# Stick-breaking attention: the sum over keys taken by parts

## The chip, the cores and the metric

The kernel runs on one NeuronCore of one Trainium2 chip. The metric is device microseconds (us) from one execution to the next of the same program. All times below are of this core; engines are named PE or TensorE (matrix products), DVE or VectorE, ACT or ScalarE, POOL or GpSimd, and SP or SyncE, whose queue issues all the kernel's DMA transfers.

## What is computed

Two layers of a decoder trunk on a sequence of 1024 tokens with 1024 channels, in float32. In each layer three groups of heads read the same stream: A (differential attention, four heads of width 128), B (forgetting attention, four heads of 64) and C (stick-breaking attention, four heads of 64). Their outputs, each times a SiLU gate, go through one output projection, and a residual and a layer norm follow. The change concerns group C, of which the reference reads, cut to what matters:

```python
def _stick_breaking_attention(q, k, v):
    ...
        strict = kpos[None, :] < qpos[:, None]
        z = jnp.einsum('bhqd,bhkd->bhqk', qb, k).astype(jnp.float32) * scale
        log_fail = jnp.where(strict, jax.nn.log_sigmoid(-z), 0.0)
        after = lax.cumsum(log_fail, axis=3, reverse=True) - log_fail
        weights = jnp.where(strict, jnp.exp(jax.nn.log_sigmoid(z) + after), 0.0)
        return jnp.einsum('bhqk,bhkd->bhqd', weights.astype(v.dtype), v)
```

With f_j = sigmoid(-z_j) and F_j the product of f over the keys from j up to the query's own position, the weight of key j is sigmoid(z_j) F_(j+1), which is F_(j+1) - F_j.

## The kernel before

**Staging.** Each layer starts with the projections of v, q and k for group C (`START`: vC0, qC0, kC0), then walks through `FOLLOW`: for each pair of heads of C (C0, C1), head of A (A0 to A3) and pair of B (B0, B1) it runs the attention and, woven into it, the projections that later units need (for C0: qC1, kC1 and vA0) and the gates of finished ones. The output projection and the norm end the layer.

**A projection** is a chain of matmuls over eight slices of 128 channels, each with three products (high and low parts of weights and stream). Its weights come by DMA into `wraw` (three buffers) and are split by ScalarE (line 133) and GpSimd (line 134). The result lands in one of two PSUM banks "acc" and is evicted by ScalarE and VectorE. v of group C is a tile of 128 partitions (position within a block) x 8 blocks x 256 columns, written block by block by ScalarE (line 212). After a q projection eight DMA transfers make copies of it with the two partition halves swapped (lines 191 and 192), which the scores need.

**Attention by blocks.** A pair of C has eight blocks of 128 queries, i = 0 to 7, with n = 128 (i + 1) keys. Each block passes three stages:

- `soft`: TensorE computes the scores (line 254, four PSUM banks "S"); for each of the two heads ScalarE takes sigmoid(-z) into f (line 369) and sigmoid(z) into w (line 370); VectorE turns f into running products from the right with a scan over the reversed row (line 372; the mask puts the 1 at the diagonal); GpSimd clears the last column of w (line 373); VectorE multiplies w by f moved one column (line 374). f and w lie in the four buffers "e", so one block takes all four.
- `turn`: TensorE transposes w in pieces of up to 512 columns into PSUM banks "T" (two banks, line 274); ScalarE copies the first piece (line 276), VectorE the second (line 278).
- `mix`: TensorE multiplies with v into a bank "T"; VectorE copies the 128 columns to y (line 390).

`LAG` makes `turn` follow one step and `mix` two steps behind `soft`. `ORDER` gives the order of the stages within one step, as indices: 0 is `soft`, 1 `turn`, 2 `mix`. For C it is (4, 3, 2, 1, 0): mix of block i-2, turn of block i-1, soft of block i. For A and B, soft comes before turn. `advance` runs one step; how often is set by the costs that the stages return (`SCORE_US`, `PACE`), against the costs of the projections woven in.

**What sets the order in the queues.** The program is written with a tile framework. It fixes each engine's queue when the program is built: among the instructions that it expects to be ready, the one written first goes first, so that one written later can be placed ahead of one that is expected to wait. On the chip each engine then works through its queue in that order. A buffer tag (`bufs`, `pbufs`) has a fixed number of slots, and a tile that takes a slot waits for the last reader of the tile before it. `tc.issue_after` holds the transposes of the output stage behind a matmul.

Of the kernel before, what the change touches and what calls it, by code (L numbers as in the profile page):

```python
# [10 lines left out]
AF = mybir.ActivationFunctionType  # L11
ALU = mybir.AluOpType
# [3 lines left out]
P = 128  # L16
D = 1024
S = 1024
NB = S // P
NK = D // P  # L20
DEPTH = 2
HALF = 512
# [18 lines left out]

PACE = 8.0
LAG = (0, 1, 2, 3, 5)
ORDER = {"A": (4, 3, 2, 0, 1), "B": (4, 3, 2, 0, 1), "C": (4, 3, 2, 1, 0)}
PARTNER = list(range(8, 16)) + list(range(8)) + list(range(16, 32))


# [1 line left out]
def tile_trunk(ctx, tc, x, ln_in_g, ln_in_b, w_in, b_forget, lambda_q1, lambda_k1, lambda_q2,  # L49
               lambda_k2, subln_g, w_out, ln_g, ln_b, c_ident, c_mask, c_tri, c_rope, out):  # L50
    nc = tc.nc
# [10 lines left out]
    def big(tag, name, shape=(P, S), dt=F32):  # L62
        return sb.tile(list(shape), dt, tag=tag, name=name, bufs=bufs[tag])

    def bank(tag, name, shape=(P, HALF)):
        return ps.tile(list(shape), F32, tag=tag, name=name, bufs=pbufs[tag])
# [6 lines left out]
    ident = const.tile([P, P], F32, name="ident")  # L73
# [4 lines left out]
    y_dram = [dr.tile([D, S], F32, name=f"y_dram{l}") for l in range(DEPTH)]  # L78
    c_dram = [dr.tile([NB * 4, P], F32, name=f"c_dram{l}") for l in range(DEPTH)]

    # ---------------------------------------------------------------- layer norm
    def pieces(n):
        return [slice(a * D // n, (a + 1) * D // n) for a in range(n)]

# [42 lines left out]
            nc.scalar.copy(hs, t3)  # L127
            nc.vector.tensor_tensor(lo[:, 4 * n:4 * n + 4, cols], t3, f32(hs), ALU.subtract)

    # ---------------------------------------------------------------- weights  # L130
    def split_w(raw, shape, key, tags):
        hi, lo = big(tags[0], f"whi_{key}", shape, F32R), big(tags[1], f"wlo_{key}", shape, F32R)
        nc.scalar.copy(hi, raw)
# [11 lines left out]
            res += [(hi[:, j, :], lo[:, j, :]) for j in range(kn)]  # L145
        return res

    # ---------------------------------------------------------------- projections
    def proj_cols(hts, w, evac, key):
        for half in range(2):  # L150
            hhi, hlo = hts[half]
# [93 lines left out]
                done(res)  # L245
        yield from proj_cols(hts, load_w(layer, col, P, key, tags=tags), evac, key)

    # ---------------------------------------------------------------- attention
    def scores(i, kst, q1, q2, key):
        half, rows = i // 4, slice((i % 4) * P, (i % 4 + 1) * P)  # L250
        res = []
# [96 lines left out]
    def attn_pair(layer, kind, pair, kst, q1, q2, v, y, negc=None):  # L348
        key = f"{kind}{layer}{pair}"
        ws, wts = {}, {}  # L350

        def soft(i):
            n = (i + 1) * P
            for s in range(2):
                k2 = f"{key}_{i}_{s}"
                sc = scores(i, kst[s], q1[s], q2[s], k2)
                if kind == "B":
                    diag = negc[s][:, n - P:n]
                    nc.gpsimd.tensor_tensor(diag, diag, mask[:, D:], ALU.add)  # L359
                    w = big("e", f"e_{k2}")  # L360
                    nm = neg_max(sc, negc[s], w, k2)
                    z = tiny.tile([P, 1], F32, tag="z2", name=f"z2_{k2}")
                    nc.scalar.activation(w[:, :n], w[:, :n], AF.Exp, bias=nm, scale=-1.0, accum_out=z)  # L363
                    nc.vector.reciprocal(z, z)
                    nc.vector.tensor_scalar(w[:, :n], w[:, :n], z, None, ALU.mult)
                else:
                    f, w = big("e", f"f_{k2}"), big("e", f"s_{k2}")
                    for a, b, p in sc:
                        nc.scalar.activation(f[:, a:b], p, AF.Sigmoid, scale=-1.0)  # L369
                        nc.scalar.activation(w[:, a:b], p, AF.Sigmoid)  # L370
                    fr = f[:, :n][:, ::-1]
                    nc.vector.tensor_tensor_scan(fr, fr, mask[:, :n], 0.0, ALU.mult, ALU.max)  # L372
                    nc.gpsimd.memset(w[:, n - 1:n], 0.0)
                    nc.vector.tensor_tensor(w[:, :n - 1], w[:, :n - 1], f[:, 1:n], ALU.mult)
                ws[i, s] = w
            return 2 * SCORE_US[i]

        def turn(i):
            wts[i] = [transposed(ws.pop((i, s)), i, f"{key}_{i}_{s}") for s in range(2)]
            return 0.22 * (i + 1)  # L380

        def mix(i):
            wt = wts.pop(i)
            o = bank("T", f"O_{key}_{i}")
            for j in range(i + 1):
                for s in range(2):
                    vc = (2 * pair + s) * 64
                    mm(o[64 * s:64 * s + 64, :P], lhsT=v[:, j, vc:vc + 64],
                                     rhs=wt[s][:, j * P:(j + 1) * P], start=j == 0, stop=j == i)
            nc.vector.tensor_copy(y[:, i * P:(i + 1) * P], o[:, :P])  # L390
            return 0.24 * (i + 1)

        order = range(NB) if kind == "C" else range(NB - 1, -1, -1)
        return [(i, soft, turn, mix, None, None) for i in order]

    # ---------------------------------------------------------------- small per-layer quantities
    def layer_scalars(layer):
        lam_init = 0.8 - 0.6 * math.exp(-0.3 * layer)
        ex = []
# [50 lines left out]
            negc.append(m.rearrange("p b s -> p (b s)"))  # L450
        return negc

    # ---------------------------------------------------------------- output projection
    OUT_ORDER = (6, 7, 0, 1, 2, 3, 4, 5)

    def load_wout(layer):
# [45 lines left out]
            nc.vector.scalar_tensor_tensor(r[:, c0:c1], r[:, c0:c1], ALPHA, acc, ALU.mult, ALU.add)  # L502
        return r

    # ---------------------------------------------------------------- the trunk
    nc.vector.memset(mhalf, -0.5)
    hts = new_ht("0")
    xs = [big("e" if blk < 4 else "K", f"x_{blk}") for blk in range(NB)]
# [36 lines left out]
    for layer in range(DEPTH):  # L545
        got, vs, ys, extra = {}, {}, {}, {}

        def project(step, tags=("whi", "wlo")):
            op, kind, n = step[0], step[1], int(step[2])
            u = step[1:]  # L550
            key = f"{op}{kind}{layer}{n}"
            if op in "qk":
                def done(res):
                    got[step] = res
                    if op == "q":
                        got["2" + u] = swapped(res, key, (1, 0) if kind == "B" else (0, 1))
                yield from proj_heads(layer, hts, COLS[op][kind] + P * n, op == "q", key,
                                      extra["rope"] if kind == "A" else None, done, tags)
            elif op == "v":
                col, width = {"C": (CV, 256), "A": (AV + P * n, 256), "B": (BV, 260)}[kind]  # L560
                fx = None
                if kind == "B":
                    xt = tiny.tile([P, NB * 4], F32, tag="fx", name=f"fx_{layer}", bufs=1)
                    fx = (xt, extra["bias"])
                vs[u] = vs[f"{kind}{n + 1}"] = yield from proj_v(
                    layer, hts, col, width, key, fx, wv0 if layer == 0 and kind == "C" else None)
                if kind == "B":
                    extra["negc"] = forget(layer, xt)
            else:
                y = ys.pop(u)  # L570
                yield from proj_gate(layer, hts, COLS["g"][kind] + P * n, y, key)
                if u != "B1":
                    e = EBASE[kind] + n
                    nc.sync.dma_start(y_dram[layer][e * P:(e + 1) * P, :], y)
                    return
                extra["ylast"] = yl = (big("wT", f"ylhi_{layer}", (P, S), F32R), big("wT", f"yllo_{layer}", (P, S), F32R))
                for a in range(2):
                    cs = slice(a * HALF, (a + 1) * HALF)
                    nc.scalar.copy(yl[0][:, cs], y[:, cs])
                    nc.vector.tensor_tensor(yl[1][:, cs], y[:, cs], f32(yl[0][:, cs]), ALU.subtract)  # L580
# [14 lines left out]
        for n, tag in enumerate(("cos", "sin")):  # L595
            t = big(tag, f"{tag}_{layer}")
# [6 lines left out]
        def advance():  # L603
            nonlocal cursor
            cost = 0.0
            for stage in ORDER[pipe[min(cursor, len(pipe) - 1)][0][0]]:
                lag = LAG[stage]
# [10 lines left out]
        for u, steps in FOLLOW.items():  # L618
            kind, m = u[0], int(u[1])
            key = f"{kind}{layer}{m}"  # L620
            q1, kst, q2 = got.pop("q" + u), got.pop("k" + u), got.pop("2" + u)
            y = ys[u] = big("y", f"y_{key}")
            if kind == "A":
                blocks = attn_a(layer, m, kst, q1, q2, vs[u], (m % 2) * P, y, nlam, sg)
            else:
                blocks = attn_pair(layer, kind, m, kst, q1, q2, vs[u], y,
                                   extra["negc"][2 * m:2 * m + 2] if kind == "B" else None)
            pipe += [(u, blk) for blk in blocks]
            fill_all = sum({"v": 21.0}.get(st[0], 10.4) for st in steps)
            attn_all = NB * PACE + 2 * sum(SCORE_US) + (0.33 if kind == "A" else 0.46) * 36  # L630
            filled = attended = 0.0
            for step in steps:
                if step[0] == "g":
                    while finished.get(step[1:], 0) < NB:
                        attended += advance()
                for cost in project(step):
                    filled += cost
                    while cursor < len(pipe) and attended / attn_all < filled / fill_all:
                        attended += advance()
            while cursor < len(pipe):  # L640
                advance()
# [5 lines left out]
        for blk in range(NB):  # L647
            key = f"o{layer}{blk}"
# [54 lines left out]
```

## Time and profile before

| | |
|---|---|
| time, median of 3 runs | 1409.74 us (1407.7 to 1410.52) |
| span of the profiled execution | 1405.8 us |
| TensorE busy | 1335.0 us (95%) |
| VectorE busy | 921.9 us (66%) |
| ScalarE busy | 600.7 us (43%) |
| GpSimd busy | 320.3 us (23%) |
| data moved by DMA | 109.28 MB on the kernel's queue |

The profile is one execution taken by the hardware profiler; its span runs from the first to the last instruction. Its own time outside the profiler was not measured apart; the median of the runs stands 3.9 us above its span. "L372" is line 372 of the kernel. In the names, buffer numbers are left out: `f_C` is every f of group C. Helpers record their lines: every matmul is L71, every transpose of `turn` L274.

### The profile page before, as it was taken

How to read it: one execution, taken by the hardware profiler on the slowest of the kernel's cores; microseconds unless marked ns; L12 is line 12 of the kernel's file. 1: busy time of each engine (PE TensorE's matmuls, PEld its weight loads, DVE VectorE, ACT ScalarE, POOL GpSimd, SP SyncE). 2: the span in 40 equal slices, each digit the busy share in tenths (PEclk: the TensorE clock that was granted, in tenths of full speed). 3: DMA queues.
4: the chain of work that ended last, by engine and by line, in shares of the span. 5: the costliest groups of instructions: out<-in, count | busy, mean ns of one | idle time of the engine just before them, and what ended most of it. 6: DMA issues, size and time to landing. Idle time of an engine off the chain costs nothing. (4 is left out here: it accounts for less than half of the span.)

```text
span 1405.8 us, 22162 instructions
## 1 busy us (share of the span) xinstructions
PE 1335.0 (95%) x8218; PEld 1134.1 (81%) x8218; DVE 921.9 (66%) x1990; ACT 600.7 (43%) x1381; POOL 320.3 (23%) x372
## 2 busy tenths in 40 slices
PE   5999989999999999999999998899999999999997
PEld 5878767987888888778898796689788888877886
DVE  7656687749775675856532657974787567757555
ACT  2445454435344544641214544544453455546200
POOL 3411211122112222223413211211111122221332
PEclk9999999999999999999999999999999999999999
DMA  7520211121213122243433111111212141232332
GB/s 266 161 76 16 56 36 53 39 75 46 61 35 103 49 76 60 91 147 121 139 108 90 46 46 39 40 51 33 80 45 62 27 113 51 71 98 98 126 129 90
DMA packets 111404, 110.70 MB, mean 79 GB/s; under 512 B 8576, under 2 KB 89408, under 8 KB 111296
## 3 DMA queue, kind: packets, MB, share of 16 engines
q1 hardware_dynamic: 111296, 109.28, 26.6%
q8 instruction: 65, 1.06, 0.3%
q14 instruction: 43, 0.35, 0.1%
HBM read 72.52 MB, written 19.96 MB: 66 GB/s over the span
## 5 line engine op out<-in xcount | busy, mean ns | idle before, releaser
L71 PE MATMUL aco_o<-wo,yhi_o 128*128 128x512 f32 (+1 forms) x462 | 142.0, 389 | 0.0
L295 ACT ACTIVATE e_A<-e_A,nm_A 128x256 f32<-128x256 f32 (+7 forms) x128 | 98.8, 773 | 31.2 <-DVE nm_A L263 30.3
L372 DVE TENSOR_TENSOR_SCAN f_C<-f_C,mask 128x128 f32<-128x128 f32 (+7 forms) x64 | 94.1, 1473 | 26.9 <-ACT f_C L369 26.7
L71 PEld LDWEIGHTS aco_o<-wo,yhi_o 128*128 128x128 f32 x462 | 85.4, 188 | 19.1
L71 PE MATMUL acr_vvA<-whi_vvA,hT 128*128 128x256 f32 x512 | 94.7, 283 | 0.0
L71 PE MATMUL aco_o<-wo,ylo_o 128*128 128x512 f32 (+1 forms) x231 | 89.7, 388 | 0.0
L71 PE MATMUL S_A<-K_kA,Q_qA 128*128 128x384 f32 (+3 forms) x384 | 85.5, 356 | 0.0
L71 PE MATMUL acc_qA<-hT,whi_qA 128*128 128x512 f32 x256 | 84.0, 408 | 0.0
L71 PE MATMUL acc_kA<-hT,whi_kA 128*128 128x512 f32 x256 | 83.5, 407 | 0.0
L71 PE MATMUL acc_ggA<-hT,whi_ggA 128*128 128x512 f32 x256 | 82.2, 400 | 0.0
L71 PEld LDWEIGHTS acr_vvA<-whi_vvA,hT 128*128 128x128 f32 x512 | 80.5, 190 | 0.3
L274 PE MATMUL T_C<-ident,s_C 128*128 128x128 f32 x288 | 51.4, 301 | 29.9 <-DVE y_C L390 27.4
L71 PEld LDWEIGHTS O_A<-v_vA,wT_A 128*128 128x128 f32 x576 | 72.3, 191 | 3.4
L71 PE MATMUL O_A<-v_vA,wT_A 128*128 128x128 f32 x576 | 74.6, 275 | 0.0
L327 ACT ACTIVATE sq_A<-ou_A 128x128 f32<-128x128 f32 x64 | 19.9, 311 | 125.2 <-DVE ou_A L316 125.1
L71 PE MATMUL acr_vvA<-wlo_vvA,hT 128*128 128x256 f32 x256 | 72.3, 282 | 0.0
L274 PEld LDWEIGHTS T_C<-ident,s_C 128*128 128x128 f32 x288 | 34.5, 150 | 44.7 <-issue 24.9
L263 DVE CUSTOM_DVE_ANT_0 e_A<-S_A,mask 128x512 f32<-128x512 f32 (+3 forms) x128 | 68.5, 554 | 2.6 <-PE S_A L71 1.1
L485 POOL TENSOR_TENSOR ylo_o<-yr_o,yhi_o 128x256 fp32r<-128x256 f32 (+2 forms) x48 | 40.6, 875 | 117.1 <-ACT yhi_o L484 114.8
L71 PEld LDWEIGHTS S_A<-K_kA,Q_qA 128*128 128x128 f32 x384 | 62.5, 189 | 4.9 <-issue 0.7
L363 ACT ACTIVATE e_B<-e_B,nm_B 128x1024 f32<-128x1024 f32 (+7 forms) x64 | 49.5, 775 | 30.7 <-DVE nm_B L263 30.7
L359 POOL TENSOR_TENSOR negc<-negc,mask 128x128 f32<-128x128 f32 x64 | 34.1, 535 | 116.6 <-DVE nm_B L263 89.3
(212 smaller groups left out, 3556.9 us busy)
## 6 DMA issues: line engine op xcount, KB each, us to landing
Q_qA<-Q_qA SPq DMA_DIRECT2D x64, 128.0 KB, 2.9
wor<-in_w_out_dram SPq DMA_DIRECT2D x32, 256.0 KB, 2.8
r_o<-h_dram SPq DMA_DIRECT2D x16, 512.0 KB, 3.2
h_dram<-x SPq DMA_DIRECT2D x8, 512.0 KB, 3.7
wr_vvA<-in_w_in_dram SPq DMA_DIRECT2D x16, 256.0 KB, 2.8
Q_qC<-Q_qC SPq DMA_DIRECT2D x32, 128.0 KB, 2.3
wr_qA<-in_w_in_dram SPq DMA_DIRECT2D x16, 256.0 KB, 2.9
wr_kA<-in_w_in_dram SPq DMA_DIRECT2D x16, 256.0 KB, 3.0
```

The costliest lines, as they stand in the source:

```text
L71: recent[0] = nc.tensor.matmul(*args, **kw).ins
L263: nc.vector.tensor_tensor_reduce(e[:, a:b], sc, other[:, a:b], -1.0, lowest, ALU.add, ALU.min, nm)
L274: nc.tensor.transpose(out=t[:, c:c + P], in_=w[:, a + c:a + c + P], identity=ident)
L295: nc.scalar.activation(e[:, :n], e[:, :n], AF.Exp, bias=nm, scale=-1.0, accum_out=z)
L327: nc.scalar.activation(t[:, b * P:(b + 1) * P], ou[:, b, :], AF.Square, scale=P ** -0.5, accum_out=ss[:, b:b + 1])
L359: nc.gpsimd.tensor_tensor(diag, diag, mask[:, D:], ALU.add)
L363: nc.scalar.activation(w[:, :n], w[:, :n], AF.Exp, bias=nm, scale=-1.0, accum_out=z)
L372: nc.vector.tensor_tensor_scan(fr, fr, mask[:, :n], 0.0, ALU.mult, ALU.max)
L485: nc.gpsimd.tensor_tensor(ylo[:, e0:e0 + en, :], raw, f32(yhi[:, e0:e0 + en, :]), ALU.subtract)
```

## The change

The sum over keys is taken by parts. Since the weight is F_(j+1) - F_j, the sum of weights times v_j is the sum over j of F_j (v_(j-1) - v_j), plus v at the query's own position, with v_(-1) = 0. So the scan's result itself is transposed and multiplied, not by v but by differences of v, and y starts as v transposed.

- `soft` of C: one sigmoid and the scan stay; the second sigmoid, the memset and the multiply go. One "e" buffer per block and head instead of two.
- `ORDER["C"]` becomes (4, 3, 2, 0, 1): in one step, soft of block i comes before turn of block i-1.
- `mix` of C multiplies with `dv` (through `vs`) and adds the PSUM block to y instead of copying it.
- The new function `by_parts` runs once per layer, right after the last instruction of the projection vC0 in the program's order (in layer 0 that generator is finished after those of q and k were run through). It takes a second "v" buffer `dv`, clears its first row, and fills it with v one position down by two DMA transfers on SP's queue: partitions 0 to 126 to partitions 1 to 127 (8 KB each), and partition 127, blocks 0 to 6, to partition 0, blocks 1 to 7 (7 KB). For each pair it transposes v (eight 128 x 128 blocks, through two "T" banks), copies it to y with ScalarE (two copies of 512 columns), and subtracts v from `dv` on VectorE (128 partitions x 8 x 128). Both y tiles of C are taken there.

```diff
-ORDER = {"A": (4, 3, 2, 0, 1), "B": (4, 3, 2, 0, 1), "C": (4, 3, 2, 1, 0)}
+ORDER = {"A": (4, 3, 2, 0, 1), "B": (4, 3, 2, 0, 1), "C": (4, 3, 2, 0, 1)}
...
                 else:
-                    f, w = big("e", f"f_{k2}"), big("e", f"s_{k2}")
+                    w = big("e", f"f_{k2}")
                     for a, b, p in sc:
-                        nc.scalar.activation(f[:, a:b], p, AF.Sigmoid, scale=-1.0)
-                        nc.scalar.activation(w[:, a:b], p, AF.Sigmoid)
-                    fr = f[:, :n][:, ::-1]
+                        nc.scalar.activation(w[:, a:b], p, AF.Sigmoid, scale=-1.0)
+                    fr = w[:, :n][:, ::-1]
                     nc.vector.tensor_tensor_scan(fr, fr, mask[:, :n], 0.0, ALU.mult, ALU.max)
-                    nc.gpsimd.memset(w[:, n - 1:n], 0.0)
-                    nc.vector.tensor_tensor(w[:, :n - 1], w[:, :n - 1], f[:, 1:n], ALU.mult)
                 ws[i, s] = w
...
-            nc.vector.tensor_copy(y[:, i * P:(i + 1) * P], o[:, :P])
+            yc = y[:, i * P:(i + 1) * P]
+            if kind == "C":
+                nc.vector.tensor_tensor(yc, yc, o[:, :P], ALU.add)
+            else:
+                nc.vector.tensor_copy(yc, o[:, :P])
             return 0.24 * (i + 1)
...
+    def by_parts(layer, v, ys):
+        dv = big("v", f"dv_{layer}", (P, NB, 256))
+        nc.gpsimd.memset(dv[0:1, 0, :], 0.0)
+        nc.sync.dma_start(dv[1:P], v[0:P - 1])
+        nc.sync.dma_start(dv[0:1, 1:NB, :], v[P - 1:P, 0:NB - 1, :])
+        for pair in range(2):
+            cs = slice(pair * P, (pair + 1) * P)
+            y = ys[f"C{pair}"] = big("y", f"y_C{layer}{pair}")
+            for half in range(2):
+                t = bank("T", f"vt_{layer}{pair}{half}")
+                for b in range(4):
+                    nc.tensor.transpose(out=t[:, b * P:(b + 1) * P], in_=v[:, 4 * half + b, cs], identity=ident)
+                nc.scalar.copy(y[:, half * HALF:(half + 1) * HALF], t)
+            nc.vector.tensor_tensor(dv[:, :, cs], dv[:, :, cs], v[:, :, cs], ALU.subtract)
+        return dv
...
                 if kind == "B":
                     extra["negc"] = forget(layer, xt)
+                elif kind == "C":
+                    vs["C0"] = vs["C1"] = by_parts(layer, vs[u], ys)
...
-            y = ys[u] = big("y", f"y_{key}")
+            y = ys[u] if kind == "C" else big("y", f"y_{key}")
+            ys[u] = y
```

## Rows read from the trace of the kernel before

**Rows 1.** The page: span, and TensorE's busy time, share, instructions.
```profile
span 1405.8 us, 22162 instructions
...
PE 1335.0 (95%) x8218; PEld 1134.1 (81%) x8218; DVE 921.9 (66%) x1990; ACT 600.7 (43%) x1381; POOL 320.3 (23%) x372
```

**Rows 2.** Windows: length, busy us (instructions) per engine, clock, DMA share, GB/s.
```profile
80.00:232.00 152.00, 137.26 (x921) 114.50 (x920) 109.64 (x142) 77.02 (x172) 25.56 (x46) 0.96 0.17 42
768.00:922.00 154.00, 138.81 (x939) 115.84 (x938) 107.45 (x142) 76.68 (x170) 26.54 (x45) 0.97 0.16 42
232.00:768.00 536.00, 527.98 (x3185) 450.94 (x3184) 336.57 (x829) 223.87 (x522) 128.40 (x131) 1.00 0.28 82
110.00:120.00 10.00, 7.21 (x51) 6.60 (x50) 7.16 (x8) 5.18 (x12) 2.69 (x3) 0.83 0.22 52
```

**Rows 3.** Waits of PE over the span: us in total, times, longest.
```profile
PE T_C L274 <- DVE y_C L390: 27.4, 16, 3.0
```

**Rows 4.** Timeline, 218 to 229 us: start, duration, engine, instruction [idle before].
```profile
218.28 2.29 DVE L372 TENSOR_TENSOR_SCAN f_C<-f_C,mask 128x1024 f32<-128x1024 f32 x1 [0.54 <-ACT f_C L369]
...
220.68 1.23 DVE L374 TENSOR_TENSOR s_C<-s_C,f_C 128x1023 f32<-128x1023 f32 x1
...
221.82 3.39 DVE L372 TENSOR_TENSOR_SCAN f_C<-f_C,mask 128x1024 f32<-128x1024 f32 x1
...
225.35 2.01 DVE L374 TENSOR_TENSOR s_C<-s_C,f_C 128x1023 f32<-128x1023 f32 x1
...
228.60 0.28 DVE L390 COPY y_C<-O_C 128x128 f32<-128x128 f32 x1
...
228.93 1.08 PE L274 MATMUL T_C<-ident,s_C 128*128 128x128 f32 x4 [3.04 <-DVE y_C L390]
```

**Rows 5.** Groups by line: count | busy us, mean ns | idle before.
```profile
L374 DVE TENSOR_TENSOR s_C<-s_C,f_C 128x127 f32<-128x127 f32 (+7 forms) x64 | 53.2, 834 | 5.4 <-ACT s_C L370 0.5
...
L370 ACT ACTIVATE s_C<-S_C 128x384 f32<-128x384 f32 (+3 forms) x96 | 49.6, 517 | 4.0 <-DVE s_C L374 4.0
...
L373 POOL MEMSET s_C<- 128x1 f32 x64 | 6.3, 99 | 210.3 <-ACT s_C L370 208.5 <-DMA Q_qA<-Q_qA 1.9
```

**Rows 6.** Timeline of PE: eight transposes in a row.
```profile
725.04 1.03 PE L124 MATMUL ht_ps_o<-ident,r_o 128*128 128x128 f32 x8
```

**Rows 7.** Groups by line and shape: VectorE's largest multiply, ScalarE's 512-column copy.
```profile
L374 DVE TENSOR_TENSOR s_C<-s_C,f_C 128x1023 f32<-128x1023 f32 x8 | 11.4, 1421 | 0.9
...
L276 ACT COPY wT_C<-T_C 128x512 f32<-128x512 f32 x40 | 23.4, 585 | 40.8 <-PE T_C L274 38.8 <-ACT wT_C L276 1.6
```

**Rows 8.** DMA: the data queue (packets, MB, share); issues by KB, us to landing.
```profile
q1 hardware_dynamic: 111296, 109.28, 26.6%
...
h_dram<-r_o SPq DMA_DIRECT2D x8, 512.0 KB, 2.6
...
c_dram<-cs SPq DMA_DIRECT2D x2, 16.0 KB, 1.4
```

**Rows 9.** Timeline of SP's queue around the ends of v, both layers.
```profile
66.24 2.86 SPq L143 DMA_DIRECT2D wr_vvA<-in_w_in_dram  x3
69.19 0.52 SPq L191 DMA_DIRECT2D Q_qC<-Q_qC  x1
...
742.00 1.63 SPq L143 DMA_DIRECT2D wr_qC<-in_w_in_dram  x2
744.50 2.81 SPq L143 DMA_DIRECT2D wr_kC<-in_w_in_dram  x2
```

**Rows 10.** Timeline of ACT: the last copies of v, both layers.
```profile
66.30 0.37 ACT L212 COPY v_vC<-acr_vvC 128x256 f32<-128x256 f32 x1
...
742.05 0.37 ACT L212 COPY v_vC<-acr_vvC 128x256 f32<-128x256 f32 x1
```

**Rows 11.** Timeline of PE: the first scores, both layers.
```profile
77.99 0.45 PE L71 MATMUL S_C<-K_kC,Q_qC 128*128 128x128 f32 x3
...
764.73 0.56 PE L71 MATMUL S_C<-K_kC,Q_qC 128*128 128x128 f32 x4
```

## The prediction

> **What bounds the kernel now.** I read the page's busy list first, then windows, then the waits of TensorE, then timelines. TensorE is busy 1335.0 of 1405.8 us [rows 1], so only its waits, its clock and the work given to it can move the time. The windows say where it waits [rows 2]: the two stretches in which group C's attention runs (80 to 232 us in layer 0, 768 to 922 us in layer 1). There TensorE is idle for 14.7 and 15.2 us, and its granted clock is 0.96 and 0.97, which is worth another 0.04 x 152 + 0.03 x 154 = 10.7 us at full speed. The 536 us between them hold 8.0 us of idle time and a clock of 1.00. So what better flow in group C can return is 29.9 + 10.7 = 40.6 us at most.
>
> Most of that idle time has one cause: 27.4 us in 16 waits of a transpose for the copy of an output block out of PSUM [rows 3], both using the two "T" banks. The copy itself is short. It is late because VectorE works in order and is behind: from 218.28 to 228.60 us it runs a scan, the multiply, a scan, the multiply and two gate steps, and TensorE waits 3.04 us for the copy at their end [rows 4]. The reader should see that the two multiplies last 1.23 + 2.01 = 3.24 us, more than the gap.
>
> **What goes.** Line 370 (96 sigmoids, 49.6 us of ScalarE), line 374 (64 multiplies, 53.2 us of VectorE) and line 373 (64 memsets, 6.3 us of GpSimd) [rows 5]. None of it is TensorE's, so it is worth only the waits that it causes. A block has two multiplies, 2 x 0.834 = 1.67 us in the mean [rows 5], and the mean gap is 27.4 / 16 = 1.71 us [rows 3]: nearly all of it would close. Against that the new order puts the scans of block i ahead of the PSUM copies of block i-1's transposes on VectorE, and those copies free the same two banks. I therefore take three quarters, 30.5 us of 40.6; the bounds are everything (40.6) and a quarter (10).
>
> **What is added, the cheap part.** Per layer 16 transposes of v: eight in a row took 1.03 us [rows 6], so 32 cost TensorE 4.2 us. Eight copies to y (0.585 us) on ScalarE and four subtractions of 1024 columns on VectorE (1.42 us by the 1023-column multiply), 10.4 us in all [rows 7], go to engines that lose 49.6 and 53.2; they cost nothing while those savings cover them, and up to their own 10.4 us if they fall in front of something that TensorE waits for. An add from PSUM in place of the copy is not in the trace; the copy takes 0.28 us [rows 4], and at twice that 32 adds would cost VectorE 9 us more, inside the 53.2 saved; I take nothing. The memset is one row on GpSimd: nothing. The second new transfer is 7 KB, about the 1.4 us of the 16 KB one [rows 8]; it hides behind the first.
>
> **What is added, the transfer.** The line that copies v one partition down moves 127 partitions x 8 KB = 1,040,384 bytes. Every transfer of the kernel before has 128, 64 or 32 partitions, so no row shows how 127 are dealt out over the 16 DMA engines. The price is bounded like this. A 512 KB transfer lands in 2.6 us and one of 16 KB in 1.4 [rows 8]; over 16 engines that is 31,744 more bytes each in 1.2 us, 26.5 KB per us for one engine, with a fixed part of about 1.4 us. Dealt over all 16 engines, the new transfer takes 1.4 + 65,024 / 26,500 = 3.9 us. On one engine it takes 1.4 + 39.3 = 40.7 us, or 58 us at the mean rate of the whole run (109.28 MB in 26.6% of 16 x 1405.8 us is 18.3 KB per us) [rows 8]; that mean is of small packets, under 1 KB each, and these rows are 8 KB, so the faster rate is nearer.
>
> Which end? Everything that the trace moves cuts into equal shares for 16 engines, and the queue's 111,296 packets are 16 x 6,956 [rows 8]. Equal shares are the only pattern I see, and 127 is a prime number: it has none but one share of 127. I take one engine, 41 us, with 0.78 for it. The Trainium skill has a rule for this, on the page "DMA: Bandwidth & Descriptors", section "Why a DMA increments its semaphore by 16 and not by 1": a transfer gets the largest number of engines, at most 16, that divides the outermost size on both sides, and 127 partitions get one. It speaks against this change; no run here has shown it yet. By it the sum is the one below; by an equal spread it is that of the second rival.
>
> **Who waits for it.** All transfers go through SP's one queue, so what is issued behind the long one and has a share on the same engine lands after it.
>
> Layer 0: v is complete at 66.7 us [rows 10], SP starts three loads at 66.24 [rows 9], and I put the new transfer behind the first of them, at about 67.2. It lands at 108. The swapped copies of q (from 69.19 on) are behind it, and the first scores stand in TensorE's queue at 77.99 [rows 11]: TensorE stops there until about 109, 31 us. Behind VectorE's subtraction, which waits as well, stand the evictions that free the projections' PSUM banks, so there is no way around.
>
> Layer 1: v is complete at 742.4 [rows 10], SP takes the two loads of 742.00 first, and the transfer goes at about 743.6, before the loads of 744.50 and the swaps of q [rows 9]. It lands at 784.3. The first scores stand at 764.73 [rows 11], which gives 21 us; if the subtraction stands ahead of q's last eviction on VectorE, k's second half finds no free bank at about 760 and the stop is 27 us. I take 24.
>
> A stop drops the clock as well: the 10 us with a gap of 2.8 us have a granted clock of 0.83 [rows 2], 1.7 us lost, so 3.4 for two stops. Together 31 + 24 + 3.4 = 58.4 us.
>
> **Sum.** 1405.8 - 30.5 + 4.2 + 58.4 = 1437.9 us of span. The median of the runs shown is 1409.74, 3.9 us above this span, which I take as what lies around it: **1442 us**. With the transfer at 40.7 to 58 us (stops of 52 to 91 us) and 40.6 to 10 us regained, this case runs from 1429 to 1498; since the ends need every bound to fall the same way, and the one-engine rate could also beat the row's, eight in ten of it lie within 1422 to 1478.
>
> **Rivals.**
> *Hidden.* The order of each engine's queue is fixed beforehand from what the framework expects of each instruction. If that expects the transfer to be long, q's swaps and the next weights go first, or projections are drawn ahead of the scores. Layer 0 then has two projections (10.4 us each by the kernel's own figure in line 629) whose weights are loaded, layer 1 one. The stops shrink to 31 - 20.8 and 24 - 10.4, together 24 us: 1441.8 - 58.4 + 24 = 1407 us, 1390 to 1425. For it: TensorE's order in this trace does mix scores, transposes and projections. Against it: the same order put transposes right where VectorE was 3 us late [rows 4], so its expectations are not exact.
> *Spread.* The transfer takes 3.9 us on all engines. It then lands before 72 us and before 748 us, ahead of the first use by any row here, and the stops vanish: 1405.8 - 30.5 + 4.2 + 3.9 = 1383.4 us, 1372 to 1400. This is the rival on the other side; it decides as soon as the transfer takes less than about 10 us, the time from 67.2 to the scores at 77.99. For it: 40 KB more than any row per engine is a bold guess from shares alone.
> *Spread, and new waits.* The transposes of block i-1 wait for PSUM copies that now stand behind two scans of up to 3.4 us [rows 4]; the 12 steps in which both blocks have over 512 columns, by 3 us each, give 36, and what is regained is gone: 1383.4 + 36, about 1419 us.
>
> **Chances.** One engine and exposed 0.66; hidden 0.12; spread 0.17; spread with new waits 0.05. About 0.2% (2.8 us) is what a measurement of this kernel can tell from no change. Faster: all but a little of the spread case and under half of the hidden one, 0.21; within 0.2%: 0.03; slower: 0.76. Range 1388 to 1480: it leaves out most of the spread case (0.13) and the upper end of the first (0.06).
>
> **What would show it.** The list of transfers: the new one's time to landing, about 41 us (right) or under 6 (wrong). The windows: TensorE idle for some 30 us from 78 and for over 20 us from 760 to 765, and a share of the DMA engines near 1/16 in those stretches. The waits: the copy of y no longer the first cause in group C, and the idle time behind 160 us and 840 us under a third of now. If VectorE is still 80% busy there, or transposes wait for their own PSUM copies, the 30.5 us were too much. The prediction is wrong if the transfer lands fast, or if it is slow and the queues have been laid around it.

## The result, and the profile after

The changed kernel takes 1468.9 us in the median (1466.2 to 1469.6, four runs), beside 1408.7 us for the kernel before on the same chip (1407.2 to 1410.5, four runs): a ratio of 1.0428, 95% interval 1.0412 to 1.0444. It is slower by 60 us. The forecast was 1442 us, inside a range of 1388 to 1480.

The page of the kernel after, its first rows; they answer to [rows 1].

```profile
span 1467.8 us, 21855 instructions
...
PE 1337.9 (91%) x8250; PEld 1134.1 (77%) x8250; DVE 868.8 (59%) x1930; ACT 565.8 (39%) x1293; POOL 307.9 (21%) x310
```

Every engine but TensorE has less to do, VectorE by 53 us and ScalarE by 35, and the span is 62 us longer. TensorE's work has grown by 2.9 us, so what grew is its waiting. The view of TensorE's waits (us in total, times, longest) says for what; it answers to [rows 3]:

```profile
PE acc_qC L71 <- DVE Q_qC L184: 35.6, 1, 35.6
PE acc_kC L71 <- DVE Q_qC L184: 35.4, 1, 35.4
PE T_C L274 <- DVE wT_C L278: 13.8, 10, 1.6
```

There are two single waits of over 35 us, one in each layer, and the 16 waits for the copy of y are gone. In their place stands a new one, ten waits for the PSUM copies of the transposes. The first two name VectorE's eviction of q, but a wait is put down to what came last. VectorE itself had waited, as its timelines in the two layers show (start, duration, engine, instruction, [idle before]):

```profile
109.15 1.23 DVE L412 TENSOR_TENSOR dv<-dv,v_vC 128x1024 f32<-128x1024 f32 x1 [52.26 <-DMA dv<-v_vC]
110.41 0.68 DVE L184 SCALAR_TENSOR_TENSOR Q_qC<-acc_qC,Q_qC 64x512 fp32r<-64x512 f32 x1
...
816.62 2.36 DVE L412 TENSOR_TENSOR dv<-dv,v_vC 128x1024 f32<-128x1024 f32 x2 [58.38 <-DMA dv<-v_vC]
```

The subtraction of the differences stands at the head of VectorE's queue and waits for the transfer of v by one partition. The evictions of q stand behind it, and TensorE needs the PSUM banks that they free. SP's timeline says when that transfer was issued, and what it did to SP itself:

```profile
65.98 0.73 SPq L402 DMA_DIRECT2D dv<-v_vC  x1
68.11 0.52 SPq L191 DMA_DIRECT2D Q_qC<-Q_qC  x1
68.69 16.85 SPq L192 DMA_DIRECT2D Q_qC<-Q_qC  x1
...
773.14 0.68 SPq L402 DMA_DIRECT2D dv<-v_vC  x1
773.91 17.20 SPq L143 DMA_DIRECT2D wr_qC<-in_w_in_dram  x1
791.21 19.72 SPq L143 DMA_DIRECT2D wr_kC<-in_w_in_dram  x2
```

From 65.98 to 109.15 us are 43.2 us, from 773.14 to 816.62 us 43.5. Right after it, issues that take about half a microsecond elsewhere take far longer: 16.85 us for a swap, 17.20 us for a load, and 19.72 us for the two loads of the last row. SP's issue itself is held. Windows of layer 0 show what moves meanwhile (length, busy us with instructions per engine, granted clock, DMA share, GB/s):

```profile
74.00:78.00 4.00, 3.59 (x20) 2.80 (x18) 0.00 (x0) 0.00 (x0) 0.00 (x0) 1.00 0.06 27
82.00:86.00 4.00, 0.00 (x0) 0.00 (x0) 0.00 (x0) 0.00 (x0) 0.00 (x0) 0.50 0.06 27
86.00:90.00 4.00, 0.00 (x0) 0.00 (x0) 0.00 (x0) 0.00 (x0) 0.00 (x0) 0.50 0.37 88
...
98.00:102.00 4.00, 0.00 (x0) 0.00 (x0) 0.00 (x0) 0.00 (x0) 0.00 (x0) 0.50 0.06 27
102.00:106.00 4.00, 0.00 (x0) 0.00 (x0) 0.00 (x0) 0.00 (x0) 0.00 (x0) 0.50 0.06 27
```

A DMA share of 0.06 is one engine of sixteen, and it moves 27 GB/s. Only from 86 us, when SP's held issue is through (85.54), do other engines have something to do; then one is left again. In this stop all four compute engines stand still. The granted clock is at 0.50, the lower of its two levels, and comes back late:

```profile
110.00:120.00 10.00, 6.78 (x22) 5.71 (x23) 5.09 (x8) 5.04 (x9) 0.00 (x0) 0.56 0.42 118
...
820.00:830.00 10.00, 8.81 (x30) 7.10 (x31) 2.48 (x4) 3.23 (x6) 2.53 (x2) 0.73 0.55 144
```

By an estimate from these two windows, 6.78 x 0.44 + 8.81 x 0.27 = 5.4 us of TensorE's work are lost to the clock; it is a little high, since the mean clock of a window counts its idle part too. Stops and clock together are 71.0 + 5.4 = 76.4 us.

### The profile page after: what moved, and what is told of

It is laid out like the page before. It is cut to its first block, busy times and chain, and to the rows that moved or that the text cites. A ratio compares the mean times of both kernels' runs of the same rounds, so it can differ in the third digit from the quotient of the medians.

```text
span 1467.8 us, 21855 instructions
## 1 busy us (share of the span) xinstructions
PE 1337.9 (91%) x8250; PEld 1134.1 (77%) x8250; DVE 868.8 (59%) x1930; ACT 565.8 (39%) x1293; POOL 307.9 (21%) x310
## 4 chain that ended last, share of the span: by engine, by line
PE 41%; DVE 5%; DMA 3%; issue 3%; ACT 1%; POOL 0%; DVEq 0%; ACTq 0%; POOLq 0%
PE aco_o L71 11%; DMA dv<-v_vC 3%; PE acc_qA L71 3%; PE acc_ggA L71 3%; PE acc_kA L71 2%; PE S_A L71 2%; PE O_A L71 2%; PE acc_kC L71 2%; PE acc_ggB L71 2%; PE acr_vvC L71 2%; PE acr_vvA L71 2%; PE acc_kB L71 2%; PE acc_ggC L71 1%; PE O_B L71 1%; PE acc_qB L71 1%
## 5 line engine op out<-in xcount | busy, mean ns | idle before, releaser
L371 DVE TENSOR_TENSOR_SCAN f_C<-f_C,mask 128x128 f32<-128x128 f32 (+7 forms) x64 | 85.5, 1376 | 31.1 <-ACT f_C L369 31.0
L71 PEld LDWEIGHTS acr_vvA<-whi_vvA,hT 128*128 128x128 f32 x512 | 79.7, 189 | 0.2
L71 PE MATMUL acc_qC<-hT,whi_qC 128*128 128x512 f32 x128 | 43.3, 415 | 36.6 <-DVE Q_qC L184 35.6
L71 PE MATMUL acc_kC<-hT,whi_kC 128*128 128x512 f32 x128 | 42.2, 410 | 35.4 <-DVE Q_qC L184 35.4
L412 DVE TENSOR_TENSOR dv<-dv,v_vC 128x1024 f32<-128x1024 f32 x4 | 4.8, 1224 | 110.7 <-DMA dv<-v_vC 110.6
L369 ACT ACTIVATE f_C<-S_C 128x384 f32<-128x384 f32 (+3 forms) x96 | 40.3, 494 | 62.8 <-PE S_C L71 62.6
```

Of the source, the lines that this page charges most:

```text
L71: recent[0] = nc.tensor.matmul(*args, **kw).ins
L369: nc.scalar.activation(w[:, a:b], p, AF.Sigmoid, scale=-1.0)
L412: nc.vector.tensor_tensor(dv[:, :, cs], dv[:, :, cs], v[:, :, cs], ALU.subtract)
```

## The experiments

Where the mix is given v in place of the differences, the text says so; its numbers are then not the reference's, while its amount of work is. A ratio is to the kernel before on the same chip, with its 95% interval.

**Is it the transfer?** The same shift in two pieces, of 112 and of 15 partitions:

```
-        nc.sync.dma_start(dv[1:P], v[0:P - 1])
+        nc.sync.dma_start(dv[1:113], v[0:112])
+        nc.sync.dma_start(dv[113:P], v[112:P - 1])
```

> The shift of v is cut in two transfers, of 112 and of 15 partitions, so that each can be dealt over many DMA engines; all else is the changed kernel. Theory A (the one transfer sits on a single DMA engine and everything behind it waits): both transfers land within 5 us, TensorE's two stops of 35.6 and 35.4 us vanish with about 6 us of clock, and the time falls from 1468.9 to about 1392 us, below the kernel before. Theory B (the stops come from the new waits as such: VectorE's subtraction behind any transfer, on a queue that others need): the stops stay over 15 us each and the time over 1430 us.

Measured: 1390.7 us, ratio 0.986 (0.983 to 0.989). That one line makes a kernel that is 4% slower into one that is 1.4% faster. The list of transfers (KB each, us to landing) and the windows of layer 0 in this kernel:

```profile
dv<-v_vC SPq DMA_DIRECT2D x2, 896.0 KB, 6.3
dv<-v_vC SPq DMA_DIRECT2D x2, 120.0 KB, 5.7
```

```profile
66.00:68.00 2.00, 2.00 (x10) 1.63 (x9) 0.00 (x0) 0.00 (x0) 1.43 (x2) 1.00 1.02 294
68.00:70.00 2.00, 2.00 (x11) 1.59 (x10) 0.00 (x0) 0.62 (x1) 1.03 (x1) 1.00 0.99 273
```

All 16 engines are at work, at up to 294 GB/s; 88% of the same bytes land in 6.3 us in place of 43, and no stop is left. The edit moves something else as well: in layer 0 the framework now places the subtraction on VectorE behind the first evictions of q and k, and not ahead of them.

```profile
78.41 0.69 DVE L182 TENSOR_TENSOR K_kC<-acc_kC,K_kC 64x512 fp32r<-64x512 f32 x1 [0.89 <-ACT K_kC L180]
...
81.27 2.34 DVE L413 TENSOR_TENSOR dv<-dv,v_vC 128x1024 f32<-128x1024 f32 x2
```

So this run alone does not part the transfer's time from the subtraction's place; the experiment without the subtraction does. The rule that the prediction drew from the Trainium skill ("DMA: Bandwidth & Descriptors", "Why a DMA increments its semaphore by 16 and not by 1") gives 127 partitions one engine and 112 all sixteen. The trace agrees: the shares are 0.06 for the one and 1.02 and 0.99 for the other.

**How does it go with the divisor?** Pieces of 124 and 3 partitions; the first divides by four:

```
-        nc.sync.dma_start(dv[1:P], v[0:P - 1])
+        nc.sync.dma_start(dv[1:125], v[0:124])
+        nc.sync.dma_start(dv[125:P], v[124:P - 1])
```

> The shift is cut in 124 and 3 partitions. If engines get equal shares, 124 goes on 4 engines (31 partitions each). Theory A: 260,096 bytes per engine at the 25 KB per us that the long transfer had (1,040,384 bytes in about 43 us) land in about 12 us, TensorE stops for 3 to 7 us per layer, time 1397 to 1408 us. Rival (a partition count that is not a multiple of 16 or 8 always goes on one engine): as the changed kernel, 1465 us. Rival (any even count is dealt over all): as with 112 and 15, about 1392 us.

Measured: 1416.9 us, one run, against 1410.1 before: between the other two as expected, but 9 us over the range. The windows and TensorE's waits:

```profile
78.00:82.00 4.00, 1.16 (x7) 0.85 (x7) 0.86 (x2) 2.87 (x4) 0.00 (x0) 1.00 0.56 115
82.00:86.00 4.00, 0.00 (x0) 0.00 (x0) 0.00 (x0) 0.00 (x0) 0.00 (x0) 0.73 0.22 68
```

```profile
PE acc_kC L71 <- DVE Q_qC L184: 11.2, 1, 11.2
...
PE S_C L71 <- DMA Q_qC<-Q_qC: 8.1, 1, 8.1
```

A share of 0.22 is about four engines of sixteen (0.25), so the dealing is as supposed. The size was off because these engines move 68 / (16 x 0.22) = 19 GB/s each, where the single one moved 27: the last of the transfer's 8 KB packets ends about 20 us after the issue in each layer, where 12 were expected. Pieces of q's swapped copies go through the same engines in this window; whether they alone make the engines slower was not settled.

**Through which wait?** The 127-partition transfer stays, but nothing reads it: no subtraction, and the mix takes v.

```
-            nc.vector.tensor_tensor(dv[:, :, cs], dv[:, :, cs], v[:, :, cs], ALU.subtract)
-        return dv
+        return v
```

> The long transfer stays, but nobody reads what it writes: the subtraction is left out and the last product takes v itself, so the output is not the reference's. It asks which of two queues made TensorE stop. Theory A1 (the queue of DMA transfers: q's swapped copies and the next weights land only after the long one): TensorE stops at the first scores or the next weights, 20 to 33 us per layer, time 1430 to 1455 us. Theory A2 (VectorE's queue alone: the subtraction holds q's eviction and with it a PSUM bank): no stop, about 1390 us.

Measured: 1462.4 us, one run, 7 us above the range. TensorE's timeline, layer 0 and then layer 1:

```profile
110.99 1.11 PE L71 MATMUL S_C<-K_kC,Q_qC 128*128 128x128 f32 x3 [31.03 <-DMA Q_qC<-Q_qC]
...
820.97 1.19 PE L71 MATMUL acc_kC<-hT,whi_kC 128*128 128x512 f32 x2 [29.97 <-DVE Q_qC L184]
```

Without a reader of the long transfer the stops stay, at 31.0 and 30.0 us. In layer 0 the scores wait for the swapped q, issued behind it. In layer 1 they never come so far: ScalarE's timeline shows that it waits for q's weights, with q's evictions behind it.

```profile
816.71 0.62 ACT L133 CAST whi_qC<-wr_qC 128x512 fp32r<-128x512 f32 x1 [34.84 <-DMA wr_qC<-in_w_in_dram]
```

The load of these weights was issued at 773.54 us, 0.8 us after the long transfer, and takes until 816.7, where such a load has a median of 3.0 to 3.7 us in the changed kernel. So the transfers queued behind make the stops by themselves; with the subtraction each stop is 4.6 and 5.4 us longer. Most of each stop is thus the transfers', whatever the subtraction's place. Whether the subtraction alone would also make stops was not run.

**Is it the queue or the engine?** As the last one, with the long transfer issued by ScalarE, in another DMA queue:

```
-        nc.sync.dma_start(dv[1:P], v[0:P - 1])
+        nc.scalar.dma_start(dv[1:P], v[0:P - 1])
...
-            nc.vector.tensor_tensor(dv[:, :, cs], dv[:, :, cs], v[:, :, cs], ALU.subtract)
-        return dv
+        return v
```

> The 127-partition transfer stays, but on ScalarE's queue instead of SP's; the subtraction is left out and the mix takes v, so the output isn't the reference's. With it on SP's queue the time was 1462.4 us and TensorE stopped 31.0 and 30.0 us for the query's swap and for wr_kC. Theory E (the one engine is held, whichever queue it came from): the swaps and weights behind it still have a sixteenth of their bytes on that engine; they share it with the long transfer packet by packet or wait for it whole, so stops of 15 to 31 us each, 1420 to 1465. Rival F (the order of SP's queue holds the others back, not the engine): no stop over 3 us, 1388 to 1394.

Measured: 1430.7 us, one run, in the range of the theory of the engine and far from the rival's; the shorter stop, 12.6 us, is under the 15 that the theory gave. TensorE's timeline, layer 0 and then layer 1:

```profile
89.01 0.66 PE L71 MATMUL S_C<-K_kC,Q_qC 128*128 128x128 f32 x2 [9.49 <-DMA Q_qC<-Q_qC]
92.79 0.45 PE L71 MATMUL S_C<-K_kC,Q_qC 128*128 128x128 f32 x1 [3.12 <-DMA Q_qC<-Q_qC]
...
781.71 1.19 PE L71 MATMUL acc_kC<-hT,whi_kC 128*128 128x512 f32 x2 [14.67 <-DVE Q_qC L184]
793.10 0.41 PE L71 MATMUL S_C<-K_kC,Q_qC 128*128 128x128 f32 x2 [2.61 <-DMA Q_qC<-Q_qC]
795.93 0.45 PE L71 MATMUL S_C<-K_kC,Q_qC 128*128 128x128 f32 x1 [2.43 <-DMA Q_qC<-Q_qC]
```

The stops are 12.6 and 19.7 us in place of 31.0 and 30.0. Another queue thus helps by about half and does not free the others. The packets that the trace holds show why. From 76 to 84 us there are 23 of 8 KB, the long transfer's, and 23 of 1 KB from SP's queue, almost strictly by turns: each small piece on the occupied engine waits for a large one. In the changed kernel, with all in one queue, there is nothing but 8 KB packets from 94 to 106 us. SP's issue is held far less here: layer 0's swaps behind the long transfer take 0.6 to 1.3 us each, and the longest row in layer 1 is this:

```profile
757.30 9.63 SPq L191 DMA_DIRECT2D Q_qC<-Q_qC  x2
```

**What did the rest of the change bring?** Only what goes, with the new order: no differences, no start value of y, a copy in place of the add; the mix takes v.

```
-            if kind == "C":
-                nc.vector.tensor_tensor(yc, yc, o[:, :P], ALU.add)
-            else:
-                nc.vector.tensor_copy(yc, o[:, :P])
+            nc.vector.tensor_copy(yc, o[:, :P])
...
-                    vs["C0"] = vs["C1"] = by_parts(layer, vs[u], ys)
+                    pass
...
-            y = ys[u] if kind == "C" else big("y", f"y_{key}")
+            y = big("y", f"y_{key}")
```

> What the change removes and reorders, alone: no second sigmoid, memset or multiply, one buffer per block and head, scores before transposes, but no shifted v, no transposes of v, no subtraction and no add (v takes the place of the differences, so the output is not the reference's). Theory A: TensorE's idle time in group C halves and its clock recovers; 15 us of idle time and 9 us of clock come back: about 1385 us. My recorded 30.5 us would give 1378. Rival (the removed work was hidden anyway): 1404 us or more.

Measured: 1389.9 us, ratio 0.986 (0.983 to 0.989), which is 19.6 us of gain, and no different from the cut transfer with everything (0.986). To part the removal from the new order, the same kernel with the order as before the change:

```
-ORDER = {"A": (4, 3, 2, 0, 1), "B": (4, 3, 2, 0, 1), "C": (4, 3, 2, 0, 1)}
+ORDER = {"A": (4, 3, 2, 0, 1), "B": (4, 3, 2, 0, 1), "C": (4, 3, 2, 1, 0)}
```

> Only the removal: no second sigmoid, no memset, no multiply, C's order of stages as before the change; no difference of values, v in its place, so the output isn't the reference's. Against 1389.9 us for removal and new order together and 1410 for the kernel before. Theory P (order matters): 1395 to 1402. Rival Q (removal alone): 1386 to 1391. A third: the removal alone does nothing, since the wait for y_C stays: 1408 to 1412.

Measured: 1374.9 us, ratio 0.9777 (0.9758 to 0.9797). All three expectations missed, each by too little gain: the removal alone brings 31.4 us, and the new order takes 11.8 of them back (about 5 either way). Group C's two stretches in this kernel, and what TensorE still waits for; the first two lines answer to [rows 2]:

```profile
80.00:232.00 152.00, 148.77 (x1028) 123.84 (x1027) 91.96 (x132) 64.69 (x137) 22.60 (x16) 1.00 0.18 46
768.00:922.00 154.00, 150.81 (x1062) 127.58 (x1061) 100.38 (x159) 66.81 (x144) 23.03 (x16) 1.00 0.19 49
```

```profile
PE T_C L274 <- ACT wT_C L276: 6.4, 8, 2.1
```

TensorE is idle for 3.2 us in each stretch, where it is 7.7 and 7.6 with the new order. The same line put back in the kernel with the cut of 112:

> The shift in two transfers of 112 and 15 partitions, and group C's blocks in the old order of stages (the turn of block i+1 before the mix of block i). With the new order T_C waited 13.8 us for VectorE's copy of wT_C behind the scan. Theory P (the new order pays for what it brought): the old order gives T_C the wait for VectorE's y_C back (27.4 us before the change, now shorter, since VectorE's multiply is gone), so 1395 us, range 1391 to 1402. Rival Q (the removal of the multiply and the second sigmoid alone did it, the new order only swapped one wait for another): 1387 to 1391, no different from 1390.7.

Measured: 1382.4 us, ratio 0.9826 (0.9806 to 0.9845). The time lies below both theories: the old order is not slower. It is faster by 5 us here, with intervals that overlap. And in the changed kernel with its whole transfer:

> The changed kernel with its 127-partition transfer, and only the order of group C's stages as before the change. With the cut transfer the old order was worth 5 to 8 us. If order and transfer are independent: 1468.9 - 7 = 1462 (1458 to 1466). Rival: the stop hides it or moves, no difference: 1467 to 1472.

Measured: 1457.3 us, ratio 1.0344 (1.0326 to 1.0363) against 1.0428: 0.84% again, 11.8 us. That is just under the range of the first theory and far from the rival's, so the long stop and the order's cost add up.

**What does the new order cost with?** In it TensorE waits ten times, 13.8 us, for VectorE's PSUM copies. One of them in the timeline of the kernel with the cut of 112:

```profile
187.20 3.40 DVE L371 TENSOR_TENSOR_SCAN f_C<-f_C,mask 128x768 f32<-128x768 f32 x2
...
190.52 0.26 DVE L278 COPY wT_C<-T_C 128x128 f32<-128x128 f32 x1
190.84 0.14 PEld L274 LDWEIGHTS T_C<-ident,f_C 128*128 128x128 f32 x1 [1.99 <-DVE wT_C L278]
190.84 0.33 PE L274 MATMUL T_C<-ident,f_C 128*128 128x128 f32 x1 [1.55 <-DVE wT_C L278]
```

A copy of 0.26 us stands behind two scans of the next block, 3.40 us, and the next transpose needs its bank. The test is to give all those copies to ScalarE, in the kernel with the cut of 112 and the new order:

```
-    def transposed(w, i, key):
+    def transposed(w, i, key, act=False):
...
-            if a == 0:
+            if a == 0 or act:
...
-            wts[i] = [transposed(ws.pop((i, s)), i, f"{key}_{i}_{s}") for s in range(2)]
+            wts[i] = [transposed(ws.pop((i, s)), i, f"{key}_{i}_{s}", kind == "C") for s in range(2)]
```

> 112 and 15 partitions, new order, and all PSUM copies of group C's turns on ScalarE. ScalarE lost 32 us of sigmoids with the change. Theory: the ten waits of T_C for VectorE's copy of wT_C (13.8 us, 1.4 each) end because a scan no longer stands ahead of that copy; 1390.7 - 13.8 = 1377, range 1376 to 1384. Rival: ScalarE's copies then queue behind each other and behind the sigmoids (T_C waits for ScalarE instead, 24 more copies of 0.5 us), 1386 to 1394.

Measured: 1375.7 us, ratio 0.9785 (0.9765 to 0.9806), within 2 us of the theory's 1377. By the ratios the gain over the cut alone is 0.9862 - 0.9785, 10.8 us (about 5 either way). The waits of T_C that are left are these, and the windows of group C's two stretches answer to [rows 2]:

```profile
PE T_C L274 <- ACT wT_C L276: 1.3, 4, 0.4
```

```profile
80.00:232.00 152.00, 151.15 (x1041) 127.24 (x1041) 86.68 (x121) 70.01 (x156) 21.71 (x16) 1.00 0.18 48
...
768.00:922.00 154.00, 153.25 (x1084) 130.95 (x1084) 93.00 (x146) 72.25 (x163) 22.24 (x16) 1.00 0.19 51
```

TensorE is idle for 0.85 and 0.75 us there, where it was 7.7 and 7.6 with the cut alone and 14.7 and 15.2 before the change, at a full clock. This is the lowest time of a version that leaves nothing out: 2.2% faster than the kernel before. With the old order on top:

> 112 and 15 partitions, the old order of group C's stages, and all PSUM copies of its turns on ScalarE: the two remedies that each took about 10 us from 1390.7 (old order alone 1382.4, ScalarE's copies alone 1375.7). If both remove the same wait (T_C for VectorE's copy of wT_C behind a scan), nothing adds up: 1374 to 1384. If the new order has a cost of its own beside that wait: 1366 to 1373. If ScalarE, which T_C waits for by 6.4 us in the old order already, becomes late: 1385 to 1395.

Measured: 1381.3 us, ratio 0.9807 (0.9790 to 0.9825), no better than the old order alone (0.9826). The two remedies go for the same wait, and in the old order ScalarE's copy is what T_C waits for, 6.7 us in 8 waits with ScalarE's copies and 6.4 us in 8 without. And the same edit in the kernel before:

> The kernel before, with nothing but all PSUM copies of group C's turns on ScalarE. There TensorE waits 27.4 us for VectorE's copy of y_C. Theory: VectorE's queue is late as a whole, so 24 copies of 0.6 us less on it shorten that wait by about half, 1394 (1388 to 1402). Rival: ScalarE still has both sigmoids here and becomes late itself: 1403 to 1415.

Measured: 1407.1 us, ratio 0.9991 (0.9978 to 1.0004): nothing, which is the rival's time, but not by its mechanism.

```profile
PE T_C L274 <- DVE y_C L390: 28.5, 16, 3.4
```

The 16 waits for y's copy stay as they were [rows 3]. Right ahead of that copy on VectorE stand two scans and two multiplies [rows 4]; the copies of the turn come before those, and taking them away (32, not the 24 of the expectation) does nothing for it.

## Why the prediction was right, and where its sizes were off

The sign and the mechanism held, and the time is 27 us above the forecast, inside its range. The two large terms were off in the same direction, so the hit is not one of errors that cancel. The parts can be read from ratios, at 1408.7 us before:

| part | predicted, us | measured, us | from |
|---|---|---|---|
| removal with the new order | -30.5 | -19.6 | 0.9861 |
| of it the removal alone | | -31.4 | 0.9777 |
| of it the new order | | +11.8 | 0.9861 - 0.9777 |
| the cheap part (transposes, y, subtractions) | +4.2 | +0.1 | 0.9862 - 0.9861 |
| 127 partitions in one transfer | +58.4 | +79.7 | 1.0428 - 0.9862 |

The measured column sums to +60.2, the predicted one to +32.1.

**One engine.** Right: a share of 0.06, 27 GB/s, and 43 us where 40.7 was worked out from the two landings in [rows 8]. Of the two rates, the one of big pieces held, and the mean of the run was far off.

**Who waits for it: the stops, 55 us in the prediction, 71.0 measured.** Both paths that it named are there, the queued transfers and the subtraction ahead of the evictions. The size is the term that was mis-sized, and it has three parts. The transfer took 2.5 and 2.8 us longer. The stop does not end when the transfer lands: VectorE's subtraction and evictions come first, from 109.15 us to TensorE's restart at 113.22 and from 816.62 to 821.19, 4 to 4.6 us that I had put at about 1. And in layer 1 I took 24 us, the middle between 21 (the first scores wait) and 27 (k's second half finds no PSUM bank). It was the bank, in both layers (q's and k's projections, not the scores), and in layer 1 it was sooner: TensorE stopped 785.8 - 773.1 = 12.7 us after the issue, where 764.73 - 743.6 = 21 us had been the cover for the scores. The clock took about 5.4 us and not 3.4. 76.4 us can be counted in the profile; the other 3.3 of the 79.7 are inside the intervals.

**What is regained, 30.5 us in the prediction, 19.6 measured.** I had taken three quarters of 40.6 because the new order puts scans ahead of PSUM copies. The quarter left out, 10.1 us, was for that order, which costs 11.8, no different within the 5 either way. What was too large is the 40.6 itself, taken as what the removal alone gives: it gives 31.4. TensorE stays idle for 6.4 us in the two stretches, with T_C waiting for ScalarE's copies, a wait that the sum had at nothing; the 2.8 us that are left are no more than the interval's half width. The order's mechanism is the one that I gave the third rival, at 1.4 us in ten waits and not at 3 us in twelve; the prediction had named transposes that wait for their own PSUM copies as the sign that 30.5 was too much. That rival's 36 us did not come: no such wait in the trace is over 1.6 us.

**The cheap part** cost nothing that could be measured with the new order. With the old order the same difference is 0.9826 - 0.9777, 6.9 us. The 4.2 us of transposes lie within the uncertainty of either, about 6 and 4 us, so the runs do not test that term closely.

**Rivals.** *Hidden* was wrong in its mechanism: the swaps of q and the weights were issued right behind the long transfer, and the subtraction was put ahead of the evictions. *Spread* was wrong of this change, where the transfer took 43 us; its "40 KB more than any row per engine" is a slip, since one engine gets 1016 KB where a transfer of 512 KB gives each 32. Its time, 1383.4 us, is that of another kernel, the one with the cut of 112 and 15 partitions: there the transfer lands in 6.3 us, under the 10 that the rival had as its point, and the time is 1390.7. The 7 us above are the smaller gain (10.9 less), of which the cheap part gives 4.1 back.

## What to carry to other kernels

A shift by one partition makes a 127 of a 128, and the time of a transfer follows how its partitions can be dealt out, not its bytes: cut off the odd rest (112 + 15), and the same copy lands in 6 us. Before an instruction is given to an engine that works in order, look at what else stands in its queue: one subtraction that waits for data holds every eviction behind it, and one scan holds a copy of a quarter of a microsecond that TensorE waits for. A change of several parts should be timed part by part: here one of them gains 31 us, one costs 12 and one costs 80, and the total says nothing about the idea.

## What the runs showed of the hardware that was not expected

- SP's own issue is held behind its own long transfer: 16.85 us for one swap and 19.72 us for two weight loads, beside 0.5 us for a swap elsewhere. With the long transfer in ScalarE's queue two swaps took 9.63 us at most, so an occupied engine alone does not account for all of it.
- One engine alone moves 27 GB/s here, four together about 19 GB/s each (share 0.22, 68 GB/s), with pieces of other transfers among them.
- A transfer on another queue still delays those of SP that have a piece on its engine: stops of 12.6 and 19.7 us beside 31.0 and 30.0 on the same queue. The two queues take turns on it, packet by packet (23 of each from 76 to 84 us).
- TensorE's clock falls to 0.50 in a stop, and in the ten microseconds around the restart its mean was 0.56 and 0.73.
